# A hybrid decoder layer on one core: the first stage's modulation slices and rows in another order, and the loads around the scan's first group moved

## The chip, the cores and the metric

The kernel runs on one core of one Trainium2 chip. The metric is the device time of one execution in microseconds (us), the median over several runs. A kernel's profile is one further execution, recorded instruction by instruction on each engine: TensorE (PE for matmuls, PEld for weight loads), VectorE (DVE), ScalarE (ACT), GpSimd (POOL), and SyncE (SP), which here only issues transfers. Times within the profile count from the span's start.

## The reference, cut to what matters

One layer for 512 prompt tokens and 8 sample tokens (520 columns together), model width 1024:

```python
mod = jax.nn.silu(c) @ w_ada + b_ada                    # 1024 -> 6*1024
sh1, sc1, g1, sh2, sc2, g2 = split(mod)
h = rmsnorm(x, norm1_w) * (1 + sc1) + sh1
proj = h @ w_in                                          # u | z | xBC | dt | gates
u, z, xbc, dt_raw, gates = split(proj)
a_out, pool_new = pool_mixer(u, ...)                     # trailing means of 2/4/8/16 tokens
xbc, conv_new = causal_conv(xbc, conv_prev, conv_w, conv_b)   # 4 taps, SiLU
dt = softplus(dt_raw + dt_bias)
y, ssm_new = ssd_scan(xh, dt, -exp(A_log), B, C, ssm_prev)    # 8 groups, chunks of 128 tokens
y = rmsnorm((y + D_skip * xh) * silu(z), ssd_norm_w) @ w_ssd_proj
x = x + g1 * ((sigmoid(gate_a) * a_out + sigmoid(gate_b) * y) @ w_out)
x = x + g2 * swiglu(rmsnorm(x, norm2_w) * (1 + sc2) + sh2)
```

The change touches the time before the second group of `ssd_scan`: the modulation `sh1, sc1`, the rows `h`, the first three column tiles of `proj`, and the start of the scan.

## The kernel before

Everything is held transposed: 128 channels on the partitions, the 520 tokens along the row. A product is done to nearly fp32 accuracy by splitting each operand into a high part (`hh`, `whi`) and a remainder (`hl`, `wlo`) and adding three products. One column tile of `w_in` (128 columns, all 1024 rows: 8 steps k, each 3 products over two halves of 260 tokens) is loaded as `raw` (512 KB, three buffers), split by ACT (L116, `whi`) and DVE (L117, `wlo`), and multiplied on PE (L129).

**First stage** (function `start`, L435). The square sums of x give `RB`, the factor of the RMS norm. The modulation weights for `sc1` and `sh1` come as five slices (`SLICES`: rows 0; 1, 2; 3, 4; 5, 6; 7), each in two transfers, through three buffers. For a slice `ada(s)` multiplies (L207) and ACT copies the sums out (`ade`, L214); `modded(s)` transposes them (L220) and makes `mod` on DVE (L225, L468). `rows(k)` makes one row tile of h: L369, L371, L372 on DVE, `hh` on ACT (L475), `hl` on DVE (L481), and has the normed x of row k + 2 made ahead (L459, even rows on DVE, odd on POOL). `products(k)` adds step k of three column tiles at once: the dt tile and the two x tiles of scan group 0, called X0(0) and X1(0). `warm(n)` multiplies zeros (L491).

**Scan.** For each group g come the column tiles X0(g), X1(g), BB(g), CC(g) and then the gate tiles ZZ of the group before; `conv` takes them out of PSUM (L642, L643 on ACT), adds the taps on DVE (L647), and a delayed part adds the sample state on POOL (L655), does tanh on ACT (L658) and the last product on DVE (L659). `conv_state` (L608, L610) prepares the sample's part from `cvs`, loaded at L599. `dt_parts` is a long chain of small DVE instructions. `dec_load(g)` (L674) loads the decay rows of a group, one row of DRAM to all partitions (1 MB), into `dec` for even groups and into a part of `aa` for odd ones; `decays` (L682 to L694) works on them on ACT. `sample(g)`, called piece by piece as `part(g)`, copies B and C of the samples out (`bcs`, L817, to `dbc` in DRAM, L818), loads states `h` and rows `cc` for four samples (L803, L804), multiplies them on POOL (L808) and sums them on DVE (L812), and then again for the other four.

**Order.** PE's order is as written throughout. From `start` to the scan's end the orders of ACT, DVE and POOL are as written too. SP's order is as written between `sp_order(True)` and `sp_order(False)` (after BB(0)), and elsewhere set by a scheduler. The list `plan` is performed item by item: `ahead(n, m)` splits the weights of the next units and issues loads for `m` more. The tiles of the scan take the place of the first stage's tiles in SBUF, so the scan's first tiles (`cvs` among them) wait for the last products.

Of the kernel before, what the change touches and what calls it, by code (L numbers as in the profile page):

```python
# [21 lines left out]
KD = 8  # L22
# [18 lines left out]
NCST = 399  # L41
NRAW = 3
URGENT = 300
WARM = 17, 7
NFS = 3
NU = 40

# [5 lines left out]
def tile_decoder(ctx: ExitStack, tc: tile.TileContext, I: dict, O: dict):  # L53
# [56 lines left out]
    def parts(raw, pool=None):  # L110
        pool = pool and G[pool]
        i = uid()
        tag = "" if pool is None else f"_{i}"
        hi = (pool or wp).tile(list(raw.shape), F32R, tag="hi" + tag, name=f"whi{i}")
        lo = (pool or wp).tile(list(raw.shape), F32R, tag="lo" + tag, name=f"wlo{i}")
        nc.scalar.copy(hi, raw)  # L116
        nc.vector.tensor_tensor(lo, raw, hi.bitcast(F32), ALU.subtract)  # L117
        return hi, lo
# [45 lines left out]
    def todo(fn, *units):  # L164
        plan.append((units, fn))

    W = {"made": [], "raws": {}}

    def ahead(n, m=0):

        queue, made, raws = W["queue"], W["made"], W["raws"]
        for i in range(len(made), min(n, len(queue))):
            u = queue[i]
            src, pool = (*u, None)[:2] if isinstance(u, tuple) else (u, None)
            with urgent() if count[0] > NU else nullcontext():
                raw = raws.pop(i) if i in raws else load(src)
                made.append(parts(raw, pool))
        for i in range(len(made), min(n + m, len(queue))):
            u = queue[i]
            if i not in raws:  # L180
                raws[i] = load(u[0] if isinstance(u, tuple) else u)

    def perform():
        queue = W["queue"] = [u for us, _ in plan for u in us]
        made = W["made"]
        at = 0
        for us, fn in plan:
            ahead(at + len(us) + (LOOK if at else 0), W.get("loads", 0))
            got = [made[at + i] for i in range(len(us))]
            for i in range(len(us)):  # L190
                made[at + i] = None
            at += len(us)
            fn(*got)
        plan.clear()
# [240 lines left out]
    def start():  # L435
        sp = st
        RB = sp.tile([P, T], F32, name="RB")
        acc = sp.tile([P, T], F32, name="acc1")
        for s in range(1, len(SLICES)):
            raws.append(ada_rows(s))  # L440
        for k in range(KD):
            add_square(sp, acc, xT[:, k], 0, T, k == 0)
        nc.vector.tensor_scalar(cwh, pv[:, PV["cw"][0] : PV["cb"][1]], 0.5, None, ALU.mult)
        ends = {}

        def ada(s, ks=range(KD)):
            m0, m1 = SLICES[s]
            n, q = P, m1 - m0
            if ks[0] == 0:
                ends[s] = bank()  # L450
            for k in ks:
                ada_mm(ends[s], raws[s][:, k], k, n, k == 0, k == KD - 1, 2 * q)
            if ks[-1] == KD - 1:
                with urgent():
                    ends[s] = ada_end(ends[s], n, lambda i: (U_SC1, U_SH1)[i // q] + m0 + i % q, sp, 2 * q)

        def normed(k):
            xn = sp.tile([P, T], F32, tag="xn", name=f"xn{k}", bufs=3)
            (nc.vector if k % 2 == 0 else nc.gpsimd).tensor_tensor(xn, xT[:, k], RB, ALU.mult)  # L459
            return xn  # L460

        def modded(s):
            m0, m1 = SLICES[s]
            with urgent():
                ends[s]()
                a1 = mod[:, U_SC1 + m0 : U_SC1 + m1]
                nw = V["n1w"][:, m0:m1].unsqueeze(2).broadcast_to([P, m1 - m0, 9])
                nc.vector.scalar_tensor_tensor(a1, a1, 1.0, nw, ALU.add, ALU.mult)  # L468

        def rows(*ks):  # L470
            hs = []
            for k in ks:
                h = sp.tile([P, T], F32, tag="h", name=f"h{k}", bufs=2)
                modulate(h, xn.pop(k), mod[:, U_SC1 + k], mod[:, U_SH1 + k])
                nc.scalar.copy(hh[:, k], h)  # L475
                hs.append(h)
            for k in ks:
                if k + 2 < KD:
                    xn[k + 2] = normed(k + 2)
            for k, h in zip(ks, hs):  # L480
                nc.vector.tensor_tensor(hl[:, k], h, hh[:, k].bitcast(F32), ALU.subtract)  # L481

        def products(k, tiles=range(3)):
            for o, w in [(outs[i], ws[i]) for i in tiles]:
                product(o, w, k, hh[:, k], hl[:, k], k == 0, k == KD - 1)


        def warm(n):
            b = bank()
            for _ in range(n):  # L490
                nc.tensor.matmul(b[:, 0:256], cold[:, 0:P], cold, start=True, stop=True)  # L491

        warm(WARM[0])
        r = rstd_start(acc, 1024, range(5))
        w0 = parts(wraw[0], "st")
        ada(0)
        modded(0)
        rstd_end(r, range(5), RB)
        warm(WARM[1])
        xn = {k: normed(k) for k in range(2)}  # L500
        rows(0)
        ws = [w0] + [parts(w, "st") for w in wraw[1:]]
        outs = [both(main()), both(main()), pair()]
        products(0, [0])
        ada(1, range(4))
        products(0, [1, 2])
        ada(1, range(4, KD))

        def rest(s):
            modded(s)  # L510
            rows(*range(*SLICES[s]))

        rest(1)
        ada(2)
        products(1)
        rest(2)
        products(2)
        ada(3)
        products(3)
        modded(3)  # L520
        ada(4)
        rows(5, 6)
        products(4)
        rest(4)
        ahead(3)
        for k in range(5, KD):
            products(k)
        first["ps"] = outs
        closed(st_)

# [135 lines left out]
    def dec_load(g):  # L666

        if g >= NG:
            return
        if g % 2:  # L670
            dec = G["aa"][:, 4:8].rearrange("p a b -> p (a b)")[:, 0:2048].rearrange("p (c h l) -> p c h l", c=4, h=4)
        else:
            dec = S["sp"].tile([P, 4, 4, P], F32, tag="dec", name=f"dec{g}")
        nc.sync.dma_start(out=dec, in_=S["dacs"][:, 4 * g : 4 * g + 4, :].unsqueeze(0).broadcast_to([P, 4, 4, P]))  # L674
        S["dec", g] = dec
# [175 lines left out]
    def sp_order(on):  # L851
        def fn():
            if on:
                fetched.__enter__()
                W["loads"] = 2
            else:
                W["loads"] = 0
                fetched.__exit__(None, None, None)

        return fn  # L860
# [61 lines left out]
    def begin(g):  # L922
        def fn():
            if g == 0:
                dec_load(0)
            dec_load(g + 1)
            gens[g] = scan(g, cur["xg"], cur["bt"], cur["ct"])
            if g:
                next(gens[g])

        return fn
# [16 lines left out]
    for g in range(NG):  # L948
        todo(x0(g), *([X0(g)] if g else []))
        if g > 1:  # L950
            todo(step(g - 1))
        if g == 2:
            todo(part(0))
        if g > 1:
            todo(part(g - 1))
        todo(x1(g), *([X1(g)] if g else []))
        if g == 0:
            todo(dt_more)
        elif g == 1:
            todo(step(0))  # L960
            todo(step(0))
            todo(part(0))
        else:
            todo(step(g - 1))
        todo(bb(g), BB(g))
        if g == 0:
            todo(sp_order(True))
            todo(dt_more)
        else:
            if g == 1:  # L970
                todo(step(0))
                todo(decay(0, 3))
            else:
                todo(decay(g))
            todo(part(g - 1))
        todo(cc(g), CC(g))
        if g == 1:
            todo(decay(0))
            todo(scores_first)
        if g:  # L980
            todo(part(g - 1))
            todo(decay(g))
            todo(zz(2 * g - 2), ZZ(2 * g - 2))
            todo(step(g - 1))
            if g == 1:
                todo(decay(1))
            todo(zend(2 * g - 2))
            todo(part(g - 1))
            todo(decay(g))
            todo(zz(2 * g - 1), ZZ(2 * g - 1))  # L990
            todo(step(g - 1))
            todo(zend(2 * g - 1))
            todo(part(g - 1))
            todo(decay(g))
        todo(begin(g))
        if g:
            todo(part(g))
        else:
            todo(flush)
# [576 lines left out]
```

## Time and profile before

| what | us |
|---|---|
| median of 3 runs (1122.76 to 1125.9) | 1124.08 |
| the profiled execution | 1125.83 |
| its span, first to last instruction | 1124.1 |
| PE busy in the span | 1081.5 (96%) |
| DVE busy | 700.8 (62%) |
| ACT busy | 463.4 (41%) |
| POOL busy | 349.0 (31%) |
| mean granted TensorE clock | 0.979 |

The profiled execution is 1.75 above the median and its span 1.73 shorter than its time, so a time on the span's scale can be read as one on the median's. PE is busy nearly always; the slices of the span that are not full lie in the first 130 us. A row of the timeline gives the start, the duration, the engine, the line and the operation; in square brackets stands how long the engine had been idle and what ended it. SPq rows are transfers at the moment of issue, with the time that the issue took.

### The profile page before, as it was taken

The numbers are of one execution on the slowest core, as the hardware profiler recorded it, in microseconds if no ns is written. First come the engines' busy times: TensorE is split into PE (matmuls) and PEld (weight loads), VectorE is DVE, ScalarE is ACT, GpSimd is POOL, SyncE is SP. The second block draws the span as 40 slices with busy tenths as digits, with TensorE's granted clock in tenths as the row PEclk, the third lists the DMA queues.
The fourth block names the chain that finished last, engine by engine and source line by source line (L and its number), as shares of the span: only waits on it lengthen the run. The fifth ranks groups of instructions, "written<-read, shape, count | busy, mean of one in ns | idle before, by whom it ended". The sixth has DMA issues, their size and how long they took to land.

```text
span 1124.1 us, 22173 instructions
## 1 busy us (share of the span) xinstructions
PE 1081.5 (96%) x9345; PEld 1052.6 (94%) x9345; DVE 700.8 (62%) x963; ACT 463.4 (41%) x774; POOL 349.0 (31%) x498
## 2 busy tenths in 40 slices
PE   7988699999999999999999999999999999999995
PEld 6888599999999999999999999899999999999995
DVE  5674778878888798789677745656455553323332
ACT  3245646646646543665333323542222222222220
POOL 1131342432442442100000000389999960000001
PEclk8999699999999999999999999999999999999997
DMA  9327335347346333454435436266666652233212
GB/s 357 145 82 198 92 125 188 110 126 189 109 127 188 120 114 108 151 172 150 150 132 166 154 117 238 97 197 217 206 208 211 190 177 83 88 88 100 85 52 76
DMA packets 58468, 165.34 MB, mean 147 GB/s; under 512 B 10881, under 2 KB 16513, under 8 KB 57601
## 3 DMA queue, kind: packets, MB, share of 16 engines
q1 hardware_dynamic: 51712, 142.96, 39.1%
q0 software_dynamic: 6656, 20.98, 6.1%
q8 instruction: 73, 1.20, 0.4%
q14 instruction: 27, 0.21, 0.1%
HBM read 151.05 MB, written 12.86 MB: 146 GB/s over the span
## 4 chain that ended last, share of the span: by engine, by line
PE 88%; DVE 3%; DMA 2%; issue 2%; ACT 2%; POOL 1%; SPq 0%; POOLq 0%; DVEq 0%; ACTq 0%
PE m L129 77%; PE b L129 4%; PE b L787 2%; DMA raw<-in_win 1%; PE b L762 1%; PE b L789 1%; PE b L301 1%; PE b L207 1%; DVE v L647 1%; PE b L740 1%; PE b L723 1%; DMA xT<-in_xT 0%; ACT whi L116 0%; DMA raw<-in_wada 0%; POOL xn L1238 0%
## 5 line engine op out<-in xcount | busy, mean ns | idle before, releaser
L129 PE MATMUL m<-hh,whi 128*128 128x260 f32 (+1 forms) x1840 | 382.4, 288 | 4.7 <-ACT v L643 3.5
L129 PE MATMUL m<-hl,whi 128*128 128x260 f32 (+1 forms) x1840 | 375.9, 285 | 3.3 <-DVE hl L481 3.1
L129 PE MATMUL m<-hh,wlo 128*128 128x260 f32 (+1 forms) x1840 | 375.6, 285 | 0.0
L117 DVE TENSOR_TENSOR wlo<-raw,whi 128x1024 fp32r<-128x1024 f32 (+2 forms) x169 | 233.7, 1386 | 183.7 <-ACT whi L116 180.8
L116 ACT CAST whi<-raw 128x1024 fp32r<-128x1024 f32 (+2 forms) x169 | 173.0, 1027 | 365.2 <-PE m L129 241.9
L129 PEld LDWEIGHTS m<-hh,whi 128*128 128x128 f32 x1840 | 287.4, 190 | 11.8 <-ACT v L643 3.7
L129 PEld LDWEIGHTS m<-hl,whi 128*128 128x128 f32 x1840 | 286.9, 190 | 4.1 <-DVE hl L481 3.8
L129 PEld LDWEIGHTS m<-hh,wlo 128*128 128x128 f32 x1840 | 287.5, 190 | 0.0
L341 POOL TENSOR_TENSOR r<-me,mhalf 128x5 f32<-128x5 f32 (+2 forms) x6 | 6.4, 1065 | 437.7 <-DVE me L340 437.7
L647 DVE SCALAR_TENSOR_TENSOR v<-xb,cwh,v 128x512 f32<-128x512 f32 x96 | 73.6, 767 | 23.1 <-ACT v L643 21.2
L129 PE MATMUL m<-ah,whi 128*128 128x260 f32 x264 | 53.3, 283 | 0.0
L129 PE MATMUL m<-ah,wlo 128*128 128x260 f32 x264 | 53.1, 283 | 0.0
L129 PE MATMUL m<-al,whi 128*128 128x260 f32 x264 | 53.0, 282 | 0.0
L129 PE MATMUL m<-gh,whi 128*128 128x260 f32 x256 | 52.9, 288 | 0.0
L1342 DVE TENSOR_TENSOR fs<-m,fs 128x520 f32<-128x520 f32 (+2 forms) x23 | 15.5, 676 | 59.1 <-PE m L129 58.3
L129 PE MATMUL m<-gl,whi 128*128 128x260 f32 x256 | 51.4, 282 | 0.0
L129 PE MATMUL m<-gh,wlo 128*128 128x260 f32 x256 | 51.3, 282 | 0.0
L1329 POOL TENSOR_TENSOR ht<-bb,xds 128x512 f32<-128x512 f32 x32 | 46.7, 1460 | 2.2 <-DMA bb<-dbc 1.7
L642 ACT COPY xb<-m 128x520 f32<-128x520 f32 (+1 forms) x31 | 17.8, 575 | 68.7 <-PE m L129 68.7
L808 POOL TENSOR_TENSOR h<-h,cc 128x1024 f32<-128x1024 f32 x16 | 38.3, 2394 | 23.2 <-DMA cc<-dbc 22.2
L1331 POOL TENSOR_TENSOR hs<-hs,ht 128x512 f32<-128x512 f32 x32 | 43.9, 1372 | 0.8
L129 PEld LDWEIGHTS m<-gh,whi 128*128 128x128 f32 x256 | 39.3, 189 | 2.1 <-PE b L301 0.9
(300 smaller groups left out, 1752.4 us busy)
## 6 DMA issues: line engine op xcount, KB each, us to landing
raw<-in_win SPq DMA_DIRECT2D x73, 512.0 KB, 4.8
raw<-in_wfi SPq DMA_DIRECT2D x44, 512.0 KB, 4.3
araw<-in_wada SPq DMA_DIRECT2D x24, 512.0 KB, 4.0
h<-in_sssm SPq DMA_DIRECT2D x16, 512.0 KB, 4.5
raw<-in_wssd SPq DMA_DIRECT2D x16, 512.0 KB, 3.4
hs<-in_sssm POOLq DMA_DIRECT2D x32, 256.0 KB, 4.1
out_ssms<-hs POOLq DMA_DIRECT2D x32, 256.0 KB, 3.6
raw<-in_wfo SPq DMA_DIRECT2D x16, 512.0 KB, 3.5
```

The lines of the kernel that those rows point to most:

```text
L116: nc.scalar.copy(hi, raw)
L117: nc.vector.tensor_tensor(lo, raw, hi.bitcast(F32), ALU.subtract)
L129: nc.tensor.matmul(o, a[:, k, c0 : c0 + P], b[:, t0:t1], start=f, stop=e)
L207: nc.tensor.matmul(ps[32 * i : 32 * i + 32, 0:n], sc[:, k], raw[:, n * i : n * i + n], start=first, stop=last)
L301: nc.tensor.matmul(ps[32 * i : 32 * i + 32, 0:256], scr[:, k], w[:, 256 * i : 256 * i + 256], start=k == 0 and j == 0, stop=k == KD - 1 an ...
L642: nc.scalar.copy(shape(xb[:, 3 + t0 : 3 + t1]), o)
L647: nc.vector.scalar_tensor_tensor(v[:, 0:TP], xb[:, k : k + TP], w(k), v[:, 0:TP], ALU.mult, ALU.add)
L787: nc.tensor.matmul(o, xdt[:, c, 2 * i + h], dec[:, c, 2 * i + h], start=c == 0, stop=False)
L808: nc.gpsimd.tensor_tensor(h0, h0, cc.unsqueeze(2).broadcast_to([P, 4, 2, P]), ALU.mult)
L1329: nc.gpsimd.tensor_tensor(t, bb.unsqueeze(2).broadcast_to([P, 2, 2, P]), at(xds), ALU.mult)
L1331: nc.gpsimd.tensor_tensor(h, h, t, ALU.add)
L1342: nc.vector.tensor_tensor(view(s[:, t0:t1]), u, view(s[:, t0:t1]), ALU.mult)
```

## The change

In `start`, all of slice 1 is multiplied right after the norm's factor, ahead of the first products; the second x tile's weights are split early and the third's after slice 1; then the three tiles of a step go together, one row is made at a time between them, and each later slice is multiplied between two steps. At its end `ahead(3, 3)` asks for three more weights. Around group 1, `dec_load(1)` and the first sample's loads are issued later, and the number of loads ahead is 2 from the first made unit on.

```diff
-WARM = 17, 7
+WARM = 17, 4
...
-    W = {"made": [], "raws": {}}
+    W = {"made": [], "raws": {}, "loads": 2}
...
-            ahead(at + len(us) + (LOOK if at else 0), W.get("loads", 0))
+            ahead(at + len(us) + (LOOK if at else 0), W["loads"] if made else 0)
...
-        w0 = parts(wraw[0], "st")
+        ws = [parts(w, "st") for w in wraw[:2]]
         ada(0)
         modded(0)
         rstd_end(r, range(5), RB)
-        warm(WARM[1])
         xn = {k: normed(k) for k in range(2)}
         rows(0)
-        ws = [w0] + [parts(w, "st") for w in wraw[1:]]
+        ada(1)
+        warm(WARM[1])
+        modded(1)
+        ws.append(parts(wraw[2], "st"))
         outs = [both(main()), both(main()), pair()]
-        products(0, [0])
-        ada(1, range(4))
-        products(0, [1, 2])
-        ada(1, range(4, KD))
...
-        rest(1)
+        products(0)
+        rows(1)
         ada(2)
         products(1)
-        rest(2)
+        rows(2)
+        modded(2)
         products(2)
+        rows(3)
         ada(3)
         products(3)
+        rows(4)
         modded(3)
+        products(4)
+        rows(5)
         ada(4)
-        rows(5, 6)
-        products(4)
-        rest(4)
-        ahead(3)
-        for k in range(5, KD):
-            products(k)
+        products(5)
+        rows(6)
+        modded(4)
+        rows(7)
+        ahead(3, 3)
+        products(6)
+        products(7)
...
-                W["loads"] = 2
...
             if g == 0:
                 dec_load(0)
-            dec_load(g + 1)
+            if g:
+                dec_load(g + 1)
...
                 todo(decay(0, 3))
+                todo(lambda: dec_load(1))
             else:
                 todo(decay(g))
-            todo(part(g - 1))
+                todo(part(g - 1))
...
         todo(begin(g))
+        if g == 1:
+            todo(part(0))
```

PE in the first stage, from slice 0's product on (`araw_117` is slice 0, `araw_132` slice 1, `araw_135` slice 2; `acc`, `r` belong to the norm; `m_260` and `m_299` are the dt tile's PSUM). Before:

```order
L207 MATMUL b_199<-araw_117,sc 32x128 x16
L220 MATMUL b_218<-cst,ade_216 128x64
L360 MATMUL b_228<-cst,r_192 128x128
L491 MATMUL b_232<-cold 128x256 x7
L129 MATMUL m_260<-hh,whi_195 128x260 x2
L207 MATMUL b_270<-araw_132,sc 32x128 x16
L129 MATMUL m_261<-hh,whi_252 128x260 x2
L220 MATMUL b_317<-cst,ade_315 128x128
L207 MATMUL b_340<-araw_135,sc 32x128 x32
```

And with the change:

```order
L207 MATMUL b_203<-araw_117,sc 32x128 x16
L220 MATMUL b_222<-cst,ade_220 128x64
L360 MATMUL b_232<-cst,r_192 128x128
L207 MATMUL b_248<-araw_132,sc 32x128 x32
L491 MATMUL b_283<-cold 128x256 x4
L220 MATMUL b_288<-cst,ade_281 128x128
L129 MATMUL m_299<-hh,whi_195 128x260 x2
L129 MATMUL m_300<-hh,whi_199 128x260 x2
L207 MATMUL b_329<-araw_135,sc 32x128 x32
```

Slice 1's whole product, the warming (four, not seven) and slice 1's transpose now stand ahead of the first step of the three tiles.

SP from the end of the first stage on. Before (`raw_556`, 562, 568 are the weights of BB(0), CC(0), X0(1); `raw_773`, 775, 794 of X1(1), BB(1), CC(1); `raw_874`, 939 of ZZ(0), ZZ(1)):

```order
L107 DMA raw_568<-in_win 128x1024
L599 DMA cvs<-in_sconv 128x1024
L107 DMA raw_773<-in_win 128x1024
L107 DMA raw_775<-in_win 128x1024
L585 DMA dtx<-dscr 64x16x8 x4
L107 DMA raw_794<-in_win 128x1024
L674 DMA dec_861<-dacs 128x4x512
L674 DMA aa<-dacs 128x4x512
L107 DMA raw_874<-in_win 128x1024
L107 DMA raw_939<-in_win 128x1024
L818 DMA dbc<-bcs_1036 16x128
L803 DMA h_0_0_1136<-in_sssm 128x1024
```

With the change (`raw_583` is X0(1); `raw_589`, 591, 593 are X1(1), BB(1), CC(1); `raw_870`, 935 are ZZ(0), ZZ(1)):

```order
L107 DMA raw_583<-in_win 128x1024
L107 DMA raw_589<-in_win 128x1024
L107 DMA raw_591<-in_win 128x1024
L107 DMA raw_593<-in_win 128x1024
L599 DMA cvs<-in_sconv 128x1024
L585 DMA dtx<-dscr 64x16x8 x4
L674 DMA dec_858<-dacs 128x4x512
L107 DMA raw_870<-in_win 128x1024
L107 DMA raw_935<-in_win 128x1024
L818 DMA dbc<-bcs_1032 16x128
L674 DMA aa<-dacs 128x4x512
L803 DMA h_0_0_1235<-in_sssm 128x1024
```

Three weights now stand ahead of `cvs`, no weight ahead of `dec`, and `aa` comes behind two weights and `dbc`.

POOL at the end of group 1. Before (`gz` are the gates of ZZ(0) and ZZ(1), `h_0_0` and `h_0_4` the sample states of group 0, `xb_1503` the input of the next group's first conv):

```order
L808 TENSOR_TENSOR h_0_0_1136<-h_0_0_1136,cc_0_1137 128x1024
L655 TENSOR_TENSOR v_1197<-v_1197,cpre 128x8
L841 COPY gz_s<-gz_1307 128x8
L841 COPY gz_s<-gz_1408 128x8
L808 TENSOR_TENSOR h_0_4_1342<-h_0_4_1342,cc_4_1343 128x1024
L638 MEMSET xb_1503 128x3
```

With the change:

```order
L655 TENSOR_TENSOR v_1190<-v_1190,cpre 128x8
L841 COPY gz_s<-gz_1303 128x8
L808 TENSOR_TENSOR h_0_0_1235<-h_0_0_1235,cc_0_1236 128x1024
L841 COPY gz_s<-gz_1400 128x8
L808 TENSOR_TENSOR h_0_4_1423<-h_0_4_1423,cc_4_1424 128x1024
L638 MEMSET xb_1500 128x3
```

The first multiplication moved behind ZZ(0)'s gate; on DVE its sum (L812) moved behind ZZ(1)'s last product (L846), and the second load of `h` on SP waits for that sum.

More of the change, by code (lines that the diff above doesn't have):

```diff
@@ L498, in start @@
         rstd_end(r, range(5), RB)
-        warm(WARM[1])
         xn = {k: normed(k) for k in range(2)}
         rows(0)
-        ws = [w0] + [parts(w, "st") for w in wraw[1:]]
+        ada(1)
+        warm(WARM[1])
+        modded(1)
+        ws.append(parts(wraw[2], "st"))
         outs = [both(main()), both(main()), pair()]
-        products(0, [0])
-        ada(1, range(4))
-        products(0, [1, 2])
-        ada(1, range(4, KD))
-        def rest(s):
-            modded(s)
-            rows(*range(*SLICES[s]))
-        rest(1)
+        products(0)
+        rows(1)
         ada(2)
         products(1)
-        rest(2)
+        rows(2)
+        modded(2)
         products(2)
+        rows(3)
         ada(3)
         products(3)
+        rows(4)
         modded(3)
+        products(4)
+        rows(5)
         ada(4)
-        rows(5, 6)
-        products(4)
-        rest(4)
-        ahead(3)
-        for k in range(5, KD):
-            products(k)
+        products(5)
[5 more added lines that the diff above has]
+        products(7)
         first["ps"] = outs
```

## The prediction

> **What bounds the kernel now.** I read the page's first part, then who waited for whom on PE, since PE is busy 96% of the span, then the windows, then the timeline of the places that the waits name. Of PE's waits from 0 to 140 us three make up most (engine, line, who released it: us in total, times, longest):
>
> ```profile
> PE b L787 <- ACT dec L693: 8.4, 1, 8.4
> PE b L815 <- ACT tok L620: 4.6, 1, 4.6
> PE m L129 <- ACT v L643: 3.5, 1, 3.5
> ```
>
> The windows show that waits are not all. Columns: stretch, its length, busy time of PE, PEld, DVE, ACT, POOL, the granted clock, the DMA share, GB/s.
>
> ```profile
> 22.20:25.60 3.40, 1.52 (x15) 1.09 (x18) 3.40 (x4) 2.52 (x3) 1.24 (x1) 0.97 1.00 419
> 25.60:29.00 3.40, 3.40 (x41) 2.96 (x34) 1.28 (x2) 0.00 (x0) 0.00 (x0) 0.53 1.01 426
> 39.20:57.30 18.10, 18.01 (x210) 16.91 (x209) 13.52 (x37) 6.32 (x10) 1.83 (x1) 1.00 0.01 5
> 90.50:93.90 3.40, 3.35 (x17) 3.38 (x18) 2.92 (x4) 2.21 (x5) 0.00 (x0) 0.54 1.01 192
> 114.40:131.10 16.70, 8.46 (x47) 6.22 (x48) 13.56 (x20) 12.44 (x29) 8.20 (x13) 0.50 0.13 41
> ```
>
> The stretch of 3.4 us in which PE worked 1.52 is followed by one at half clock (0.53), so thin work costs twice. The transfers are full (419 and 426 GB/s) until 29 us. From 39.2 on PE is busy throughout. The change works on three places: the first stage to 57.3, the wait at L815, and the wait at L787.
>
> **The first stage.** Its rows: the warming after `RB`, slice 2's product, the last step of the products, BB(0)'s first product; and the issue to landing of slice 1's first half (issued at 10.06):
>
> ```profile
> 19.09 3.19 PE L491 MATMUL b<-cold 128*128 128x256 f32 x14
> 31.26 1.95 PE L207 MATMUL b<-araw,sc 128*32 128x128 f32 x64
> 55.17 0.40 PE L129 MATMUL m<-hh,whi 128*128 128x260 f32 x2
> 57.32 0.41 PE L129 MATMUL b<-hh,whi 128*128 128x260 f32 x2
> ...
> araw<-in_wad SPq DMA_DIRECT2D x1, 1024.0 KB, 10.3
> ```
>
> A step costs 57.32 - 55.17 = 2.15 at full clock, a two-row slice 1.95 (its halves 0.98), one warming matmul 3.19 / 7 = 0.46. Slice 1's first half lands at 10.06 + 10.3 = 20.4, and at 426 GB/s each further MB takes 2.46: second half 22.9, slice 2 by 27.8, slice 3 by 32.7. PE is free for slice 1 at 19.1, where the warming stood. It does the first half at 20.4 to 21.4, the second at 22.9 to 23.9, four warmings (1.8) to 25.7 and the transpose (0.3, an estimate): products begin at 26.0, but then nothing is late: 8 steps x 2.15 + slices 2 to 4 at 1.95 + three transposes at 0.25 = 23.8, so they end at 49.8. Cover: slice 2 is needed at 28.2, slice 3 near 34.6; DVE must give a row per 2.15 to 4.1 us, and a row costs it 2.0: from 39.2 to 57.3 it worked 13.52, of which three `wlo` took 3.50 (next part), on five rows. One thing I take off: between 18.8 and 22.2 PE would work 0.4 + 1.0 = 1.4 us, as thin as the stretch that was followed by 0.53. Then the second half takes 2.0 and two of the warmings run at half clock: 1.3 later, 51.1. Gain: 57.3 - 51.1 = **6.2** (bounds: 8.3 if slice 1 is whole at 21.5 and the clock stays; 4.5 if one more stretch falls to half clock, 1.7).
>
> **`cvs` behind three weights.** These are the rows from `cvs` to the wait at X1(1):
>
> ```profile
> 53.82 3.50 DVE L117 TENSOR_TENSOR wlo<-raw,whi 128x1024 fp32r<-128x1024 f32 x3 [0.25 <-ACT whi L116]
> 57.56 0.33 SPq L599 DMA_DIRECT2D cvs<-in_sconv  x1
> 61.24 0.76 POOL L608 TENSOR_TENSOR cpre<-cvs,cwh 128x256 f32<-128x256 f32 x1 [3.50 <-DMA cvs<-in_sconv]
> 61.84 6.14 DVE L647 SCALAR_TENSOR_TENSOR v<-xb,cwh,v 128x512 f32<-128x512 f32 x6 [2.03 <-ACT v L643]
> 67.28 0.64 ACT L658 ACTIVATE t<-v 128x520 f32<-128x520 f32 x1 [4.09 <-POOL v L655]
> 77.43 0.78 ACT L643 ACTIVATE v<-m,cwh 128x520 f32<-128x520 f32 x1 [0.91 <-DVE xg L659]
> 78.27 0.51 PE L129 MATMUL m<-hh,whi 128*128 128x260 f32 x2 [3.48 <-ACT v L643]
> ```
>
> `cvs` went out 0.25 after the last product. Now X1(1)'s, BB(1)'s and CC(1)'s weights stand ahead of it in SP's queue, each waiting for a buffer that the three `wlo` (3.50) free. The last row tile is ready some 2 us before the products' end (with its `mod` only after step 5), so the three `wlo` end 2 us after it (before, at 57.32, with it), and `cvs` is issued 2.45 after the end: 2.2 later. With 512 KB just ahead in the queue (1.26, worked out below) it lands 2.2 to 3.1 later. There is no slack: POOL's chain ended as DVE's six `v` did (67.28 + 0.64 against 61.84 + 6.14), and from L659 on DVE is busy until `xg` at 77.4. Against it, the `v` took 6.14 for 6 x 0.77 = 4.6 beside POOL's L608 and L610; apart, both are quicker, up to 1.5. I take **-2.3** (bounds -1.5, -3.1): PE's wait at X1(1) grows from 3.5 to 5.8.
>
> By the row at 90.5 a wait of 4.6 brought 3.4 us at 0.54, while X1(1) ran at full clock after 3.5. With 5.8 it may run at half clock for one such stretch, 1.7 us; I charge nothing, since the next part shows what hides it. The Trainium skill, TensorE: Matmul & The Clock Gate, What's actually happening, says that the gate looks at free-running windows of about 3.4 us and halves the clock after an idle one, so a wait of 5.8 cannot get away with it; the trace agrees in the length (rows of 3.40 at 0.53 and 0.54). By that rule and without cover the sum would be 1114.1 in place of 1112.4.
>
> **The wait at L815 and ACT's 9 us.** Times of this part are those of before, counted from X1(1)'s start at 78.27. Rows of SP, ACT and PE, then the landing of `raw_794`, `dec`, `aa` and `raw_874`:
>
> ```profile
> 83.06 1.08 SPq L107 DMA_DIRECT2D raw<-in_win  x1
> 84.25 0.49 SPq L674 DMA_DIRECT2D dec<-dacs  x1
> 85.36 1.90 SPq L107 DMA_DIRECT2D raw<-in_win  x2
> 88.98 1.04 ACT L116 CAST whi<-raw 128x1024 fp32r<-128x1024 f32 x1 [4.15 <-DMA raw<-in_win]
> 89.93 0.47 ACT L620 COPY tok<-b 128x384 f32<-128x384 f32 x1
> 90.55 0.37 PE L815 MATMUL b<-cst,bc_s 128*16 128x128 f32 x1 [4.61 <-ACT tok L620]
> 101.76 1.05 ACT L116 CAST whi<-raw 128x1024 fp32r<-128x1024 f32 x1 [9.05 <-DMA raw<-in_win]
> 113.61 0.37 ACT L765 COPY hst<-b 128x256 f32<-128x256 f32 x1
> 120.48 0.69 PE L787 MATMUL b<-dec,xdt 128*64 128x128 f32 x4 [8.37 <-ACT dec L693]
> ...
> raw<-in_win SPq DMA_DIRECT2D x1, 512.0 KB, 5.9
> dec<-dacs SPq DMA_DIRECT2D x1, 1024.0 KB, 9.8
> aa<-dacs SPq DMA_DIRECT2D x1, 1024.0 KB, 15.7
> raw<-in_win SPq DMA_DIRECT2D x1, 512.0 KB, 16.4
> ```
>
> CC(1)'s weight was issued at 83.06, landed at 88.96 and kept ACT from `tok`, and so PE from L815. Asked for 25 us earlier it is there: ACT, idle for 4.15 before 88.98, splits it at 84.83, `tok` ends 1.04 + 0.47 later at 86.35, PE waits some 0.5, and BB(1), eight steps of a third of 2.15 and a transpose, ends at 92.5 at full clock. `dec` landed at 94.05, `aa` (issued at 84.8) at 100.5 and `raw_874` at 101.76: one after another, 1.26 for a weight. Now neither `raw_794` nor `aa` is ahead of ZZ(0)'s weight: `dec` lands at 94.05 - 1.3 = 92.8, the weight at 94.0, and ACT goes on there and not at 101.76. From there to L765 and L787 the queues of ACT, DVE and POOL are as before (the decays, CC(1)'s conv, the states one after the other), so L787 comes 7.8 earlier. In PE's terms: wait 4.6 to 0.5, half clock 3.4 x 0.46 = 1.5 regained, and L787's wait 8.4 to 6.3; together 7.7, the same. **+7.8** (bounds: 9.3, where BB(1)'s end at 92.5 holds ACT; 5.5, if `dec` alone keeps the weight 2.3 longer). A half-clock window in X1(1) puts BB(1)'s end at 94.2, and ACT is still in the weight's split until 95.0: that is why it costs nothing here.
>
> **What is late next.** `aa` is issued behind two or three weights; ACT reads it first after all of group 0's decays, that is behind L787's release, near 113, and 1 MB more behind the weights that land at 94 to 97 is there by 104. The sample's first multiplication no longer stands in POOL's way; the second (L808 on `h_0_4`) does:
>
> ```profile
> 129.95 1.21 DVE L812 TENSOR_REDUCE y_s<-h 128x8 f32<-128x1024 f32 x1
> 131.24 0.33 SPq L803 DMA_DIRECT2D h<-in_sssm  x1
> 136.46 2.41 POOL L808 TENSOR_TENSOR h<-h,cc 128x1024 f32<-128x1024 f32 x1
> 137.39 2.02 DVE L846 SCALAR_TENSOR_TENSOR y<-gz,y 128x512 f32<-128x512 f32 x1
> 143.96 2.33 DVE L647 SCALAR_TENSOR_TENSOR v<-xb,cwh,v 128x512 f32<-128x512 f32 x3 [1.60 <-ACT v L643]
> 156.10 1.89 PE L762 MATMUL b<-xde,bm 128*128 128x256 f32 x8
> ```
>
> Its load now waits for L812 after L846, to 140.6; `cc` lands as late after it as before (136.5 - 131.2 = 5.2), 145.8, POOL is done at 148.2, and the next conv on DVE, whose input POOL clears behind it, starts there and not at 144.0: a slip of some 4 us. PE first reads from that chain at L762 at 156.1, 12 us after the conv's start, of which DVE and POOL need about 9 by the order (a conv, the two scalings); so nothing (bounds 0 and -2). The three warmings less are PE time that is idle time otherwise; no other work changes.
>
> **Sum.** 6.2 - 2.3 + 7.8 = 11.7 off the span of 1124.1: 1112.4. The execution itself took 1125.83, 1.73 more, and the median of the runs, 1124.08, lies 1.75 below it; so 1112.4 for the median too.
>
> **Rivals.** (1) The first stage gives little: slice 1 ahead of the products leaves PE idle until 22.9, and two or three more stretches fall to half clock, 1.7 each. For it: the thin stretch at 22.2 was followed by 0.53. Against it: from 26.0 PE's queue holds no wait. First stage 2 in place of 6.2: 1116.6. (2) The weights around `dec` go out together, not in turn, so ZZ(0)'s weight lands near 97.5: +4.3 in place of 7.8, 1115.9. For it, only 192 GB/s moved while `dec` and `aa` were under way; against it, the landings stand in order. (3) More than I take: the first stage keeps its clock (1.3), ACT goes on at 92.8 (1.2), and the clock comes back before the gate tile that ran at half clock from 127 to 131.1 (2.0): 1107.9. (4) X1(1) runs at half clock after its longer wait and nothing hides it (the weight lands early, BB(1) late): one stretch of 3.4 at half clock, 1.7: 1114.1. For it, the row at 90.5; against it, the split until 95.0. (5) The other side: `cvs`. If it lands as late as a weight did in the crowded stretch, 16.4, and three weights of 1.26 on top, that is 20.2 after the issue, 18.8 later than before, and the DVE chain takes all of it: 1124.1 - 6.2 - 7.8 + 18.8 = 1128.9. It decides from 14.0 on. Against it: only 1.5 MB is ahead, with no broadcast rows. (6) No change, 1124: the places gain, but the wait at L787 grows by what L815's loses; this needs ACT's chain to be held by something other than the weight, and ACT's idle row names nothing else.
>
> DMA: Bandwidth & Descriptors, Queues, rings and completion order, of the Trainium skill, says that one queue's descriptors are taken in ring order on each engine. It speaks against (2) and for the delay of `cvs`; the landings at 88.96, 94.05, 100.5 and 101.76 agree.
>
> **How the numbers follow.** Forecast 0.56; (1) 0.12; (2) 0.09; (3) 0.10; (4) 0.06; (5) 0.03; (6) 0.04. The range takes (1) to (4) and the bounds: best 8.3 - 1.5 + 9.3 and the clock's 2.0 would be 1106.0; worst 4.5 - 3.1 + 5.5 - 1 = 5.9, 1118.2. I give 1106 to 1118. About 0.3% is what a measurement can tell from no change here: faster 0.93, same 0.04, slower 0.03.
>
> **What would show it.** BB(0)'s first product near 51, none of the rows at 0.53 between 29 and 51; PE's wait at X1(1) near 5.8 with POOL's L608 released by `cvs`; the wait at L815 under 1 and ACT's `whi` after `bcs` no longer 9; L787's wait near 6.3. Wrong would be: a first product tile after 27.5, waits for `araw`, `dec` landing after ZZ(0)'s weight, or new PE waits beyond 140 us.

## The result and the profile after

The changed kernel took 1115.28 us (median; 1115.1 to 1116.7) against 1124.17 beside it: ratio 0.9923, 95% interval 0.9906 to 0.994. Measured once more, beside the other kernels, it took 1115.73 against 1123.62, 0.9935 [0.9911, 0.996]. The profiled execution took 1115.18, its span 1113.4.

PE's waits from 0 to 140 us (who was waited for: us in total, times, longest):

```profile
PE b L787 <- ACT dec L693: 7.3, 1, 7.3
PE m L129 <- ACT v L643: 6.5, 1, 6.5
PE b L207 <- DMA araw<-in_wad: 2.0, 2, 1.6
...
PE b L787 <- DVE dec L748: 1.1, 1, 1.1
```

The wait at L815 is gone, the one at X1(1) (L129) has nearly doubled, the one at L787 is 1.1 shorter. Windows of the first stage and of X1(1) (columns as before: stretch, length, PE, PEld, DVE, ACT, POOL, granted clock, DMA share, GB/s):

```profile
18.40:21.80 3.40, 1.81 (x33) 1.59 (x35) 3.08 (x8) 0.65 (x2) 1.84 (x2) 0.81 1.03 436
21.80:25.20 3.40, 2.98 (x48) 2.17 (x41) 2.42 (x3) 1.34 (x3) 1.25 (x1) 0.68 1.01 424
25.20:28.60 3.40, 3.40 (x29) 3.08 (x27) 2.12 (x8) 0.50 (x1) 0.00 (x0) 1.00 1.01 424
...
75.20:78.60 3.40, 3.40 (x16) 3.40 (x17) 3.19 (x5) 0.64 (x1) 1.38 (x5) 0.51 0.09 6
```

The half clock that stood at 25.6 to 29.0 has moved ahead of the products, into slice 1, and a new one follows the wait at X1(1). PE's timeline: slice 1's halves, warming, the first product, BB(0)'s first product, X1(1), L787 twice, and a wait far behind:

```profile
20.46 1.92 PE L207 MATMUL b<-araw,sc 128*32 128x128 f32 x32 [1.59 <-DMA araw<-in_wad]
22.80 1.61 PE L207 MATMUL b<-araw,sc 128*32 128x128 f32 x32 [0.42 <-DMA araw<-in_wad]
24.34 1.99 PE L491 MATMUL b<-cold 128*128 128x256 f32 x8
26.20 0.49 PE L129 MATMUL m<-hh,whi 128*128 128x260 f32 x2
51.26 0.41 PE L129 MATMUL b<-hh,whi 128*128 128x260 f32 x2
75.19 0.80 PE L129 MATMUL m<-hh,whi 128*128 128x260 f32 x2 [6.47 <-ACT v L643]
111.66 0.69 PE L787 MATMUL b<-dec,xdt 128*64 128x128 f32 x4 [7.32 <-ACT dec L693]
113.50 1.90 PE L787 MATMUL b<-dec,xdt 128*64 128x128 f32 x12 [1.14 <-DVE dec L748]
407.66 0.50 PE L129 MATMUL m<-plh,whi 128*128 128x260 f32 x2 [0.98 <-ACT ub L1030]
```

SP, DVE, POOL and ACT for the two waits:

```profile
50.67 2.90 SPq L107 DMA_DIRECT2D raw<-in_win  x3
53.74 0.33 SPq L599 DMA_DIRECT2D cvs<-in_sconv  x1
55.78 5.05 DVE L647 SCALAR_TENSOR_TENSOR v<-xb,cwh,v 128x512 f32<-128x512 f32 x6 [2.03 <-ACT v L643]
59.54 0.75 POOL L608 TENSOR_TENSOR cpre<-cvs,cwh 128x256 f32<-128x256 f32 x1 [7.87 <-DMA cvs<-in_sconv]
64.22 0.64 ACT L658 ACTIVATE t<-v 128x520 f32<-128x520 f32 x1 [7.08 <-POOL v L655]
74.36 0.78 ACT L643 ACTIVATE v<-m,cwh 128x520 f32<-128x520 f32 x1 [0.91 <-DVE xg L659]
80.09 0.94 SPq L674 DMA_DIRECT2D dec<-dacs  x1
81.14 4.24 SPq L107 DMA_DIRECT2D raw<-in_win  x2
92.93 1.05 ACT L116 CAST whi<-raw 128x1024 fp32r<-128x1024 f32 x1 [7.36 <-DMA raw<-in_win]
```

and the transfers, with KB and us from issue to landing:

```profile
cvs<-in_sconv SPq DMA_DIRECT2D x1, 512.0 KB, 5.7
...
dec<-dacs SPq DMA_DIRECT2D x1, 1024.0 KB, 10.7
```

`cvs` goes out behind three weights, 2.5 after BB(0)'s first product began, and takes 5.7 where it took 3.6; DVE is through with its six `v` at 60.8 and waits for POOL. `dec` takes 10.7 from its issue, to 90.8, and ACT stands idle until ZZ(0)'s weight lands 2.1 behind it.

Five marks in PE's timeline cut every trace of this study in the same pieces: the start of BB(0)'s first product, of X1(1), of L787 with its wait, of the next row of sixteen at L787, and L330 on `sqlast` near the end. The first column is a time, the others are the lengths between the marks; three kernels were traced twice.

| kernel | to BB(0) | to X1(1) | to L787 | to sixteen | to `sqlast` |
|---|---|---|---|---|---|
| before | 57.32, 55.80 | 20.95, 21.00 | 42.21, 42.58 | 14.33, 12.93 | 975.1, 974.7 |
| changed | 51.26, 50.30 | 23.93, 24.11 | 36.47, 36.87 | 12.49, 13.11 | 975.7, 975.9 |
| first stage alone | 50.27 | 22.09 | 42.60 | 13.52 | 976.3 |
| scan part alone | 55.58 | 23.31 | 37.23 | 12.08 | 974.5 |
| `cvs` ahead | 51.22 | 21.06 | 35.56 | 12.79 | 976.2 |
| weight ahead of `dec` | 52.52 | 24.19 | 33.60 | 12.60 | 977.1 |
| both | 51.17 | 21.02 | 33.64 | 12.09 | 975.9 |
| `aa` behind `dec` | 51.30 | 23.95 | 41.88 | 13.08 | 976.5 |
| sample part early | 52.28, 51.75 | 24.15, 24.25 | 36.44, 35.93 | 13.44, 13.77 | 976.4, 976.5 |
| warming added | 50.28 | 23.80 | 36.09 | 13.38 | 976.0 |
| all edits together | 50.90 | 20.93 | 33.60 | 13.03 | 975.6 |

In the means of the two traces each the change gains 5.8 in the first stage, loses 3.0 up to X1(1), gains 5.7 up to L787 and 0.8 behind it, and loses 0.9 after that: 8.4, where the medians fell by 8.9 and 7.9.

### The profile page after: what moved, and what is told of

Read it like the earlier page. It is cut to its first block, busy times and chain, and to the rows that moved or that the text cites. A ratio compares the mean times of both kernels' runs of the same rounds, so it can differ in the third digit from the quotient of the medians.

```text
span 1113.4 us, 22158 instructions
## 1 busy us (share of the span) xinstructions
PE 1074.8 (97%) x9339; PEld 1047.2 (94%) x9339; DVE 695.9 (63%) x963; ACT 463.6 (42%) x774; POOL 347.5 (31%) x498
## 4 chain that ended last, share of the span: by engine, by line
PE 87%; DMA 3%; DVE 3%; issue 2%; POOL 2%; ACT 2%; SPq 0%; POOLq 0%; DVEq 0%; ACTq 0%
PE m L129 76%; PE b L129 4%; PE b L787 2%; PE b L762 1%; DMA araw<-in_wad 1%; DMA raw<-in_win 1%; PE b L789 1%; PE b L301 1%; POOL xn L1241 1%; PE b L740 1%; PE b L723 1%; DMA xT<-in_xT 1%; DMA cvs<-in_sconv 1%; DVE wlo L117 0%; PE b L207 0%
## 5 line engine op out<-in xcount | busy, mean ns | idle before, releaser
L129 PE MATMUL m<-hh,whi 128*128 128x260 f32 (+1 forms) x1840 | 380.9, 287 | 7.6 <-ACT v L643 6.5
L129 PE MATMUL m<-hl,whi 128*128 128x260 f32 (+1 forms) x1840 | 374.2, 284 | 0.5 <-DVE hl L481 0.2
L129 PE MATMUL m<-hh,wlo 128*128 128x260 f32 (+1 forms) x1840 | 373.9, 283 | 0.0
L129 PEld LDWEIGHTS m<-hh,whi 128*128 128x128 f32 x1840 | 285.9, 189 | 13.8 <-ACT v L643 6.7
L129 PEld LDWEIGHTS m<-hl,whi 128*128 128x128 f32 x1840 | 285.4, 189 | 1.1 <-DVE hl L481 0.7
L129 PEld LDWEIGHTS m<-hh,wlo 128*128 128x128 f32 x1840 | 285.7, 189 | 0.0
L129 PE MATMUL m<-ah,whi 128*128 128x260 f32 x264 | 53.2, 283 | 0.0
L129 PE MATMUL m<-ah,wlo 128*128 128x260 f32 x264 | 53.1, 282 | 0.0
L129 PE MATMUL m<-al,whi 128*128 128x260 f32 x264 | 53.0, 282 | 0.0
L129 PE MATMUL m<-gh,whi 128*128 128x260 f32 x256 | 52.8, 288 | 0.0
L129 PE MATMUL m<-gl,whi 128*128 128x260 f32 x256 | 51.3, 282 | 0.0
L129 PE MATMUL m<-gh,wlo 128*128 128x260 f32 x256 | 51.3, 282 | 0.0
L808 POOL TENSOR_TENSOR h<-h,cc 128x1024 f32<-128x1024 f32 x16 | 39.7, 2481 | 29.7 <-DMA cc<-dbc 27.7
L658 ACT ACTIVATE t<-v 128x520 f32<-128x520 f32 x32 | 20.4, 637 | 51.7 <-POOL v L655 51.7
```

The lines of the kernel that those rows point to most:

```text
L129: nc.tensor.matmul(o, a[:, k, c0 : c0 + P], b[:, t0:t1], start=f, stop=e)
L658: nc.scalar.activation(t, v, AF.Tanh, bias=0.0, scale=1.0)
L808: nc.gpsimd.tensor_tensor(h0, h0, cc.unsqueeze(2).broadcast_to([P, 4, 2, P]), ALU.mult)
```

## The experiments

**Each half of the change alone.** The first keeps only the order in `start` (with `WARM`); the second keeps only the rest:

```diff
# first stage alone, against the changed kernel
-        ahead(3, 3)
+        ahead(3)
...
-            if g:
-                dec_load(g + 1)
+            dec_load(g + 1)
...
-                todo(part(g - 1))
+            todo(part(g - 1))
# scan part alone, against the kernel before
-        ahead(3)
+        ahead(3, 3)
```

> The changed first stage alone; around the scan's first group everything stands as in the kernel before. Theory: the parts of the change add up, and the first stage is worth 6.0 us of the span (the first product of BB(0) came at 51.28 after the change, 57.32 before). Then BB(0) begins near 51.3, cvs is issued about 0.3 behind the last product, PE's wait at X1(1) is again near 3.5, the wait at L815 4.6 and the wait at L787 8.4, and the time is about 6 us under before: 1118. Rival: what the first stage saves is given back at a later wait that does not move with it (the rows of dec and aa, issued by the clock of the loads): then the waits at L815 and L787 grow by up to 6, and the time is 1121 to 1124.

> The scan's part alone (weights asked for ahead, aa and the sample's loads later), with the first stage of before. Theory: additive, -2.9 at cvs, +5.7 from X1(1)'s start to L787, +1.8 behind L787 (what the two traces show): about 4.6 under before, 1119.5. PE's wait at X1(1) between 5 and 6.5, at L815 under 1, at L787 near 7.3, and cvs issued some 2 us behind the last product. Rival: with the first stage of before the three wlo end with the products and not behind them, so cvs is hardly late; then the wait at X1(1) is 3.5 to 4.5 and the gain 6.5 to 7.5, 1117.

Measured: the first stage alone 1120.53, ratio 0.9967 [0.9955, 0.9979], so 3.7 by the ratio (4.4 by the medians) and not 6; the scan part alone 1119.46, 0.9954 [0.9937, 0.9972], 5.2 (5.5), the theory's 1119.5. Together that is 8.9 (9.8), where the whole change gave 7.9 and 8.9: within intervals of 1.3 to 2 us to each side the halves add up, and nothing shows that one eats the other's gain. In the scan part alone `cvs` was issued 0.5 after BB(0)'s first product began, as the rival had it, and still landed 6.7 later, so the wait was 5.9, as the theory had it: what costs is the place behind the three weights, not the late issue. PE's waits of the first stage alone:

```profile
PE b L787 <- ACT dec L693: 10.1, 1, 10.1
PE m L129 <- ACT v L643: 4.6, 1, 4.6
PE b L815 <- ACT tok L620: 3.1, 1, 3.1
```

The rival had both L815 and L787 growing; L787 grew by 1.7 as L815 shrank by 1.5, and to L787 the piece is as long as before (42.60). So nothing is given back there. The shift between the two waits is not the edit's: the kernel before has 1.8 and 10.3 in its second trace. There, and in the first stage alone, X1(1) ran at half clock and PE came later to L815; in the first trace of before X1(1) ran at full clock. What lacks to 6 is 1.1 up to X1(1) (22.09; `cvs` landed 4.3 after its issue, for 3.6) and, against the traces of before, 1.2 to 1.6 in the last column, of which 0.98 is the same wait at ACT's `ub` near 410 as in the changed kernel; the rest is the first column, next.

**The kernel before, traced again.**

> The kernel before, a second trace, for the end of its first stage: 57.32 in the first trace, whose execution lay 1.7 above the median, but 55.58 with the same first stage in the run of the scan's part alone. If the stage varies by where the half clock falls, this one ends between 55.5 and 57.5, and the first stage's worth is 4 to 6, not 6.2 in every run; if it ends at 57.3 again the lesser gain of the first stage alone has another cause.

BB(0) began at 55.80, and the first reading of the expectation holds: the stage varies. Its windows from 18.40, to be set beside 22.20 to 29.00 of the first trace, where a thin stretch was followed by one at 0.53:

```profile
18.40:21.80 3.40, 3.04 (x15) 2.39 (x12) 0.91 (x4) 0.91 (x3) 0.49 (x1) 0.59 1.01 427
21.80:25.20 3.40, 2.74 (x13) 1.93 (x11) 3.33 (x5) 1.51 (x3) 2.60 (x2) 1.00 1.02 424
25.20:28.60 3.40, 2.55 (x43) 2.21 (x44) 3.07 (x4) 1.01 (x2) 0.00 (x0) 1.00 1.02 431
```

Here the half clock fell ahead of the thin stretch, into the warming, where it cost less. Three traces with the old first stage put BB(0) at 57.32, 55.80 and 55.58, nine with the new one at 50.27 to 52.52, median 51.26. Against that median the first stage is worth 4.3 to 6.1, by which old trace is taken. The runs do not say which is the typical one: the execution with 57.32 lay 1.75 above its kernel's median, the two others 1.3 and 1.5 below theirs.

The spread of the new stage lies wholly ahead of the products. From the first product to BB(0) it takes 25.04 to 25.08 in all eleven traces that have it (the two with added warming too); the first product begins between 25.22 and 27.45. Two things are seen to move it: the half clock (it lasts until 26.3 in the latest trace), and when slice 1 lands (PE begins on its first half at 20.0 in the earliest traces, but at 21.51 in one that had no half clock after 19.0 and began its products at 26.71).

**`cvs` ahead of the three weights.**

```diff
-        ahead(3, 3)
+        ahead(3)
...
         nc.sync.dma_start(out=cvs, in_=I["sconv"])
+        ahead(3, 3)
```

> The changed kernel with cvs asked for ahead of the three weights (X1(1), BB(1), CC(1)) instead of behind them; else unchanged. Theory: the weights ahead of cvs in SP's queue are the whole of the loss at X1(1). Then cvs is issued within 0.5 of the last product and lands 3.6 later, PE's wait at X1(1) falls from 6.5 to about 3.5, X1(1) runs at full clock, dtx and dec and all behind them move with it, and the time falls by 2.9, to 1112.4. Rival: the wait at X1(1) falls but ZZ(0)'s weight, which ACT waits for, comes no earlier, or X1(1)'s own weight now comes late: the wait at L787 grows by as much, 1114.5 to 1115.5.

Measured 1112.51, 0.9897 [0.9879, 0.9915], the theory's 1112.4. Its rows (one line is added, so L643 is L644 here):

```profile
51.46 0.33 SPq L599 DMA_DIRECT2D cvs<-in_sconv  x1
51.89 2.47 SPq L107 DMA_DIRECT2D raw<-in_win  x3
55.30 0.75 POOL L609 TENSOR_TENSOR cpre<-cvs,cwh 128x256 f32<-128x256 f32 x1 [3.67 <-DMA cvs<-in_sconv]
72.28 0.80 PE L129 MATMUL m<-hh,whi 128*128 128x260 f32 x2 [3.60 <-ACT v L644]
```

`cvs` arrives 4.2 earlier, X1(1) 2.9, and the whole 2.8. The order in SP's queue was the whole loss. One point fell: X1(1) ran at half clock here too (0.80 for a pair of matmuls against 0.51), after a wait of 3.60.

**ZZ(0)'s weight ahead of `dec`, and both edits.** `W.update(loads=3)` stands ahead of CC(1)'s unit and `loads=2` behind it, which lets one more weight out:

```diff
+        if g == 0:
+            todo(lambda: W.update(loads=3))
         todo(cc(g), CC(g))
+        if g == 0:
+            todo(lambda: W.update(loads=2))
```

> The changed kernel with ZZ(0)'s weight asked for ahead of dec (one weight more is let out ahead before CC(1)); else unchanged. Theory: what my 7.8 lacked is that ACT still waits 7.4 for that weight, behind dec's 1 MB. With the weight ahead of dec, ACT's wait at whi goes under 5 and ends no later than BB(1)'s products (90.1 in the changed kernel's trace), and L787's wait falls from 7.3 by up to 2.9; dec lands 1.3 later. Time 1112.4 to 1113.5. Rival: dec itself is needed as soon as the weight is (the decays read it first), so that the wait moves from the weight to dec and the time stays within 1 us of the changed kernel's 1115.3.

> The changed kernel with both edits: cvs ahead of the three weights, and ZZ(0)'s weight ahead of dec. Theory: they act at two waits in a row and add, 2.9 at X1(1) and up to 2.9 at L787: 1109.5 to 1111. Rival: with the weight out of the way dec is late, and what X1(1) gains is given back there: no better than the better of the two alone, 1112.4 or above.

Alone: 1115.36, 0.9916 [0.9901, 0.9931], no gain in the median against the changed kernel: the time missed the theory's range and is the rival's, but the trace does not show the rival's mechanism, a wait moved to `dec`: ACT now waits for PE and not for a transfer,

```profile
92.17 0.59 ACT L642 COPY xb<-m 128x520 f32<-128x520 f32 x1 [3.83 <-PE m L129]
```

and from X1(1) to L787 it takes 33.60 where the changed kernel took 36.47 (L787's wait is 4.0 for 7.3): the 2.9 is there. Its first column is the latest of all (52.52), and its last one the longest (977.1), 1.3 and 1.4 more than in the changed kernel's trace, in stretches that the edit does not touch. Both together: 1110.44, 0.9875 [0.986, 0.989], 2.1 under `cvs` alone, and the piece is 33.64 again. In the traces the two edits add, up to L787; in the time the second one's part is less sure, since alone it showed nothing and with `cvs` 2.1, with intervals that overlap.

**`aa` behind `dec` again.**

```diff
-            if g:
-                dec_load(g + 1)
+            dec_load(g + 1)
...
-                todo(lambda: dec_load(1))
```

> The changed kernel with aa (1 MB of broadcast rows) asked for right behind dec again, as before, ahead of ZZ(0)'s weight. Theory: the queue works in turn, so ZZ(0)'s weight lands some 6 later than in the changed kernel (aa landed 6.4 behind dec before), ACT's wait of 7.4 at whi becomes about 13, and L787 comes 5 to 6 later: 1120 to 1121.5. That would make aa's move nearly the whole of the 5.7. Rival: dec, aa and the weight share the engines, and the weight comes only 2 to 3 later: 1117 to 1118.

Measured 1122.49, 0.9982 [0.9971, 0.9992]: 7 lost, 1 more than the theory's range. SP and ACT:

```profile
80.16 1.02 SPq L674 DMA_DIRECT2D dec<-dacs  x1
81.22 2.12 SPq L674 DMA_DIRECT2D aa<-dacs  x1
83.38 3.53 SPq L107 DMA_DIRECT2D raw<-in_win  x2
98.41 1.04 ACT L116 CAST whi<-raw 128x1024 fp32r<-128x1024 f32 x1 [12.79 <-DMA raw<-in_win]
```

ACT waits 12.8 (expected 13), L787 comes 5.5 later, and the piece, 41.88, is nearly that of the kernel before. So moving `aa` out of the weight's way is nearly the whole gain at L787; the weights asked for ahead empty the wait at L815, but without `aa`'s move L787 takes that back.

**The sample's part early again.**

```diff
-                todo(part(g - 1))
+            todo(part(g - 1))
...
-        if g == 1:
-            todo(part(0))
```

> The changed kernel with the sample's part of group 0 back in its old place, ahead of CC(1): the first load h_0_4 is issued early and POOL's L808 runs early again. Theory: the 1.8 that came behind L787 (my forecast had 0) came from POOL's L808 leaving DVE's three L748 alone (2.93 before, 1.90 after) and the wait behind them (2.17 before, 1.14 after): the time rises by 1 to 1.8, to 1116.3 to 1117.1, and the row of L748 is near 2.9 again. Second effect to be seen: h_0_4 in the queue ahead of dec or the weight makes the wait at L787 longer, up to 1.3 more. Rival: the 1.8 is the granted clock's alone, by when the long wait ends; then L748 slows and the time does not change by more than 0.5.

> The changed kernel with the sample's part of group 0 in its old place, once more, since 3.8 was measured where its trace shows 1.0 (L748 2.86 with its wait against 1.84). If the rest was a bad draw of the first stage and of the stage at 700 to 750 us, the time is 1 to 2 above the changed kernel's on this chip. If it belongs to the edit it is 3 to 4 again, and the granted clock is 0.978 to 0.981 in all runs where the changed kernel has 0.982 to 0.986.

First 1119.1, 0.9956 [0.994, 0.9973], outside the theory's range; then 1116.73, 0.9936 [0.9915, 0.9958], beside 1115.73, 0.9935, of the changed kernel, which is no difference by the ratios. The traces show 1.0 at L787 both times; DVE and POOL in the first:

```profile
112.78 2.35 POOL L808 TENSOR_TENSOR h<-h,cc 128x1024 f32<-128x1024 f32 x1
113.96 2.93 DVE L748 TENSOR_TENSOR dec<-dec,cbm 128x512 f32<-128x512 f32 x3 [1.19 <-ACT dec L694]
```

Beside POOL's L808 the three L748 take 2.93 (one of them 1.72, the others 0.7 or less); in the changed kernel, without it, 1.90, and L787's second row waits 1.1 and not 2.2. The Trainium skill, SBUF — State Buffer, Who interferes with whom, says that a VectorE instruction with two inputs in SBUF contends with a GpSimd instruction that reads SBUF, and that the ports they share are locked exclusively; both runs agree, in the size of about 1 us. The wait at L787 was not longer, so `h_0_4` ahead of `dec` costs nothing. Why the first measurement lay 3.8 above the changed kernel's is only partly seen (a first column 1.0 later, and a granted clock of 0.978 to 0.981 in all its runs); the second, at 0.978 to 0.986, did not repeat it.

**Warming ahead of slice 1, and all edits together.**

```diff
         rows(0)
+        warm(3)
         ada(1)
```

> The changed kernel with three more warming matmuls ahead of slice 1 (1.4 us of PE time from 18.9, in which PE waits for araw until 20.5). Theory: the half clock from 20.3 on (granted 0.50 to 0.53 until 23.9, slice 1's second half took 1.61 where 0.98 is full speed) follows the idle stretch 18.9 to 20.5; with PE busy there the clock stays and the products begin 0.6 to 1.3 earlier, the whole 0.6 to 1.3 shorter, if slices 2 and 3 still land in time. Rival: the stretch until 22.8 stays thin whatever stands before it, since the second half's araw lands at 22.8; then the half clock stays or comes later, and the products begin within 0.3 of 26.2.

> All three edits on the changed kernel: cvs ahead of the three weights, ZZ(0)'s weight ahead of dec, three warming matmuls ahead of slice 1. Theory: the first two add (2.9 at X1(1), 2.5 behind it, as the two together gave 1110.4 and the changed kernel 1115.3), and the warming takes away the bad draws of the first stage (its products' end lay between 50.3 and 52.5 in seven traces of the same code, by where the half clock fell), 0 to 1: about 1110, ratio to the kernel before 0.987. Rival: the added warming delays slice 1 in some runs, and the time is 1110.5 to 1112.

> The changed kernel once more, beside the others on the same chip: 1115 to 1116, with the first product of BB(0) between 50.3 and 52.5 in its trace.

The warming alone: 1115.02, 0.9916 [0.9899, 0.9932], the changed kernel's time. In its trace both halves of slice 1 run at full speed (1.08 each) and BB(0) begins at 50.28; but the first stage alone, without the added warming, had 1.08 and 50.27 too. It may take away bad draws; this many runs cannot show it. With the other two edits: 1109.4, 0.9865 [0.984, 0.989], beside 1115.73 for the changed kernel. That is the best version here, some 6 under the changed kernel; its third edit is not shown to do anything in the time.

## Why the prediction was right, and where not

The forecast of 1112.4 lay 2.9 to 3.3 below the medians of 1115.3 and 1115.7, inside the range, and the chain of causes was the one described. Step by step:

- **First stage, +6.2.** The signs came: first product at 26.20, BB(0) at 51.26 for a predicted 51.1, nothing at half clock from 29 to 51. That it came out so close is luck: inside it two errors met. I had the products begin at 27.3 (26.0 and 1.3 for the clock, though the two parts that I named, 1.0 for the half slice and 0.9 for two warmings, make 1.9) and take 23.8; they began 1.1 earlier, since the half clock took only 0.5 off the second half and nothing off the warmings, and took 25.06. This size is no draw, it is 25.04 to 25.08 in every trace: I priced all steps at 2.15, the last one's, while the eight with their transposes took 19.4 and not 17.95. The base is weak too. I took 57.32 from an execution 1.75 above its median and let 1.73 and 1.75 cancel, as though the excess lay outside the parts that change. Against the second trace, 1.5 of it lies in this one and 1.4 behind L787. So the term is 4.3 to 6.1, in or just under the lower half of my bounds, 4.5 to 8.3.
- **`cvs`, -2.3.** The issue came 2.48 after the products' end (predicted 2.45) and the wait was 6.5 for 5.8. The term measured -3.0. Mis-sized was the landing: 5.7 instead of 3.6 behind three weights, not one, so that POOL's L608 began 4.4 later and not 2.2 to 3.1 (and my 2.2 and 1.26 make 3.5, not 3.1); the quicker `v` (5.05 for 6.14, as foreseen) could not make that up, since DVE waited for POOL.
- **Half clock at X1(1).** It came (0.51) and was hidden, as argued: in the changed kernel BB(1)'s products end at 90.05, before the weight. It is no mark of the longer wait, though: the kernel before has it in its second trace after 3.53.
- **L815 and ACT, +7.8.** L815's wait went altogether, L787's fell to 7.3 for 6.3. The term measured 5.7. The failed step is `dec`'s landing at 92.8: I let it land 1.3 earlier because `raw_794` no longer stands ahead of it. From its issue it took 10.7 where it had taken 9.8, and the weight came 2.1 after it, not 1.26. Over all traces it takes 9.8 to 10.8 with a weight just ahead of it and 10.2 to 11.0 without one, so there was nothing to take off. That is near the lower bound, 5.5, "if `dec` alone keeps the weight 2.3 longer". The rest of the step held: from `whi` to L787 18.73, as before.
- **Late next, 0.** The later second half of the sample's part cost nothing that the traces show. I overlooked that the same move leaves L748 alone on its ports: 1.0 less wait at L787, shown in the traces by putting it back. And a new wait, 0.98 at 407.66, stands ahead of `ub`: 0.47 to 1.79 in the nine traces of the new first stage without added warming, and in none of the old. The last column is some 1 longer in all eleven, so about as much is given back; but the two with added warming have the longer column without this wait, so it is not the whole cause. Both stay open.

By rivals: in size the first stage and the weight behind `dec` lie between the forecast and (1) and (2), but not by their mechanisms: nothing fell to half clock behind the first product, and with `aa` put back ahead of it the weight came 5.4 later, so the loads are served in turn. (4)'s half clock came and was hidden. (3), (5) and (6) are out.

## What to carry to other kernels

Ask of each load which wait it ends, and order the queue by that: here 512 KB behind three weights cost 3 us, and 1 MB that nobody needed yet, ahead of a weight that ACT stood waiting for, cost 5 to 7. When a transfer leaves a crowded queue, do not credit the next one with its whole share: bound it by its own time from issue to landing. And before a stage's length is taken from one trace, look where the half clock fell in it: a second trace of the old kernel would have taken 1.5 off the first stage's term.

## What the runs showed of the hardware

PE's wait at X1(1) was between 3.47 and 4.62 in six traces, and the first row behind it tells the clock (about 0.5 for two matmuls at full clock, 0.80 at half). In the kernel before (second trace):

```profile
76.80 0.80 PE L129 MATMUL m<-hh,whi 128*128 128x260 f32 x2 [3.53 <-ACT v L643]
```

and in the best version:

```profile
71.83 0.52 PE L129 MATMUL m<-hh,whi 128*128 128x260 f32 x2 [3.47 <-ACT v L645]
```

After 3.47 and 3.48 (the first trace of before) the clock stayed; after 3.53, 3.56, 3.60 and 4.62 it was halved. It looks like a fixed length of idle time, but the traces speak for a matter of phase. In each trace all changes of the granted clock lie whole multiples of 3.41 us apart (a half clock lasts 3.41 or 6.83 at X1(1)), and this grid lies differently from trace to trace. The second trace of before around its wait of 73.27 to 76.80, then the first trace of before (74.79 to 78.27) and the best version (68.36 to 71.83), cut along the grid:

```profile
72.36:75.77 3.41, 0.90 (x8) 0.69 (x6) 3.31 (x6) 1.92 (x4) 0.00 (x0) 1.00 0.07 19
75.77:79.18 3.41, 2.38 (x11) 2.38 (x12) 3.22 (x6) 1.42 (x2) 2.19 (x5) 0.50 0.02 1
...
73.16:76.57 3.41, 1.63 (x14) 1.42 (x12) 3.23 (x7) 1.92 (x4) 0.00 (x0) 1.00 0.07 19
76.57:79.98 3.41, 1.72 (x14) 1.72 (x15) 3.25 (x6) 1.42 (x2) 2.19 (x5) 1.00 0.01 1
...
66.67:70.08 3.41, 1.69 (x14) 1.47 (x13) 3.20 (x8) 1.92 (x4) 0.00 (x0) 1.00 0.07 19
70.08:73.49 3.41, 1.66 (x13) 1.67 (x14) 3.25 (x6) 1.43 (x3) 2.19 (x5) 1.00 0.01 1
```

The clock was halved 2.5 us into the first of these waits, behind a stretch in which PE had worked 0.90. The other two waits are as long, but each is shared by two stretches with some 1.7 of work, and the clock stayed. In the twelve traces with half clock at X1(1) the stretch ahead of it held 0 to 1.2 us of PE's work. How little is too little does not follow: stretches with 1.5 to 2.5 went either way elsewhere. The Trainium skill, TensorE: Matmul & The Clock Gate, What's actually happening, says that the windows of about 3.4 us run freely, so that the point of transition varies from run to run. The grid agrees with that. By that rule a wait of 5.8 need not hold a whole window, and my prediction was wrong to say that it cannot get away; here all eight waits of 5.85 to 6.78 brought half clock all the same, and the half clock behind 0.90 of work shows that a stretch need not be idle throughout.
